# Both triangular solves of the chunked delta rule in rooms of their own, block and bias-row loads on GpSimd, modulation pieces in pairs

## The chip, the cores and the metric

One core of a Trainium2 chip runs the whole program: TensorE (PE) multiplies, VectorE (DVE) and ScalarE (ACT) work on elements, GpSimd (POOL) sets memory and copies, SyncE (SP) issues most of the loads and stores. The metric is the device time of one execution in microseconds (us); the median of several is compared.

## The reference, cut to what matters

The model is a backbone of two layers over 256 latent tokens and 256 context tokens, 2048 wide. Every layer has a mixer and a gated feed-forward block (FFN), each with a shift, a scale and a gate that come from the conditioning vector c. The part of the first layer's mixer that the change touches is a delta rule that runs over chunks of 64 tokens in both directions, first over the context ("ctx", without an output), then from its final states over the latent tokens ("own" below):

```python
sh1, sc1, g1, sh2, sc2, g2 = jnp.split(silu(c) @ ada_w[l] + ada_b[l], 6, axis=-1)
m = jnp.where(i[:, None] > i[None, :], jnp.einsum('bhnid,bhnjd->bhnij', kb, k) * decay, 0.0)
t_inv = lax.linalg.triangular_solve(eye + m, eye, left_side=True, lower=True, unit_diagonal=True)
...
def step(s, xc):
    v_new = u_c - w_c @ s
    s_next = s * jnp.exp(gl_c) + kd_c.T @ v_new
    return s_next, (None if q is None else qd_c @ s + a_c @ v_new)
...
o_c, s_ctx_fin = gdn_bidirectional(None, k_c, v_c, g_c, beta_c, (zeros, zeros))
o_l, _ = gdn_bidirectional(q_l, k_l, v_l, g_l, beta_l, s_ctx_fin)
y_na = neighbourhood_attention(qb, kb, vb, k_ctx_na, v_ctx_na, rpb)     # scores + rows of rpb
y = jnp.concatenate([norm(o_l) * silu(za), y_na], axis=-1) @ w_out
```

All of it is in float32. A product with a weight is made of three matmuls on halves of the operands: high times high, low times high, high times low.

## The kernel before, in words

**The weight stream.** Weights are loaded by SyncE in pieces of 128x1024 (`raw`), split by ACT (`whi`, line 176) and by the DVE (`wlo`, line 250), and used by matmuls at lines 303, 304, 308, 320 and 348. The first layer's stream runs through the segments KA, QA, VA (keys, queries, values of the delta rule), KB0, VB0, KB1, VB1 (keys and values of the attention heads, in halves), QB0, QB1 (their queries), ZA (gate of the delta rule) and WO (output projection); then comes the FFN. One `wlo` serves 24 weight matmuls of the stream up to ZA. "Weight matmul n" or "split n" below counts from the start of this stream.

**The other work** stands in a plan and is fed between the weight matmuls at a pace for each segment: `R_KB` for KB and VB, `R_QB`, `R_ZA`, `R_WO`. `P_CH` and `P_INV` say at which place of the plan the steps of the delta rule begin. The numbers set the program order of each engine, and every engine works through its own order without overtaking.

**The delta rule** goes like this, for ctx and then for own:

- `chunk_matrices` computes the 16 triangular matrices (lines 984 to 1009), cuts out the 32x32 diagonal blocks (`dgs`), the neighbours of size 32 (`n32`, copied by GpSimd at line 1006) and of size 64 (`n64`, by ACT), sends them through DRAM (`nd64`, `nd32`, `dl`), and solves all diagonal blocks at once on the DVE in 31 dependent steps (lines 1030 to 1034, on `lsol` and `zsol`). The solution and its transpose go to DRAM (`dz`).
- `load_diag` sets two tiles to zero on GpSimd (`xd`, `xdT`; lines 1053, 1054) and loads four 32x32 blocks of 16 matrices into each (line 1059, by SyncE): 64 KB a load, in pieces of 32 floats.
- `inverses` builds the inverse of the 128x128 matrices out of the blocks, with small matmuls (lines 1085, 1092, 1098; tiles `gd`).
- `scan` runs the recurrence (lines 1123 to 1167) on `state`.

Tiles with the same tag share room, and the later one waits until the earlier one is no longer read. `nt` (a chunk's matrix) and `lsol` share one room between ctx and own, as do `dgs`, `zsol` and `xd` under the tag "diag".

**Beside it.** `ada_mixer` computes 12 rows of 512 modulation values, each as a sum over 16 pieces: SyncE loads a piece (`araw`, 256 KB, line 433) up to six ahead, the DVE adds it to `acc` (line 438), whose first row was loaded with the bias. A matmul with ones closes a row (line 445). The attention heads need rows of `rpb` as bias: `bq`, loaded by SyncE in two halves for a head (line 1307). GpSimd loads `hC`, a part of the modulated input, in seven loads (line 1276) in the stream's half VB1.

Of the kernel before, what the change touches and what calls it, by code (L numbers as in the profile page):

```python
# [29 lines left out]
D = 2048  # L30
# [12 lines left out]
KH = 2  # L43
P_CH = 2
P_INV = (16, 22, 50, 56)
AB = 6
AHEAD = 6
LAG = 3
LATER = 2
R_QB = 0.6  # L50
R_KB = 1.6
R_ZA = 2.0
R_WO = 2.0
NST = 3
# [58 lines left out]
def body(tc, x, c, ctx, c_ctx, ada_w, ada_b, norm_mix, norm_ffn, ffn_w_gate, ffn_w_up, ffn_w_down,  # L113
# [240 lines left out]

    def ada_done(l, seg, kind, gamma, fs_, p):

        if kind == "sc":
            DVE.scalar_tensor_tensor(scc[l, seg - 1][:, fs_], p, 1.0, gamma[:, fs_], op0=OP.add, op1=OP.mult)
        else:
            DVE.tensor_copy((shc if kind == "sh" else gcol)[l, seg][:, fs_], p)  # L360
# [54 lines left out]
    def ada_mixer(pool_, parts):  # L415


        wr = ada_w[0].rearrange("(k p) n -> p k n", p=128)
        blocks = [(seg, kind, gamma, b) for seg, kind, gamma in parts for b in range(4)]
        accs, raws = {}, {}  # L420

        def load(i):
            n, k = divmod(i, KT)
            if n >= len(blocks):
                return
            seg, b = blocks[n][0], blocks[n][3]
            c0 = seg * D + b * 512
            if not k:
                acc = accs[n] = pool_.tile([128, 512], F32, name="acc", tag="acc", bufs=2)
                DVE.memset(acc, 0.0)  # L430
                SP.dma_start(acc[0:1, :], ada_b[0:1, c0:c0 + 512])
            raws[i] = pool_.tile([128, 512], F32, name="araw", tag="araw", bufs=AB)
            SP.dma_start(raws[i], wr[:, k, c0:c0 + 512])

        def total(i):
            n, k = divmod(i, KT)
            with tc.issue_after(last_lo[0]):
                DVE.scalar_tensor_tensor(accs[n], raws.pop(i), cT[:, k:k + 1], accs[n], op0=OP.mult, op1=OP.add)  # L438

        def close(n):  # L440
            seg, kind, gamma, b = blocks[n]
            acc = accs.pop(n)
            p = smt()
            for f in range(4):
                PE.matmul(p[:, f:f + 1], acc[:, f * 128:(f + 1) * 128], ones[:, 0:1], start=True, stop=True)
            ada_done(0, seg, kind, gamma, slice(b * 4, b * 4 + 4), p[:, 0:4])
            if kind == "row" and b == 3:
                p = smt()
                transpose(p[0:16, 0:128], gcol[0, seg])
                g = pool_.tile([16, 128], F32, name="grow", tag="araw", bufs=AB)  # L450
                DVE.tensor_copy(g, p[0:16, 0:128])
                SP.dma_start(row_d[0, seg], g)

        for i in range(AHEAD):
            load(i)
        N = len(blocks) * KT
        for i in range(N + LAG):
# [109 lines left out]
    ACT.dma_start(vrow[64:112, :], od_conv.rearrange("o t (k p) -> (o t k) p", p=128))  # L567
    brow = sp.tile([32, 128], F32, name="brow")
    bT = sp.tile([128, 32], F32, name="bT")
    ACT.dma_start(brow, ada_b[0:1, 0:4096].rearrange("o (r p) -> (o r) p", p=128))  # L570
    ACT.dma_start(erow, ev_conv.rearrange("o t (k p) -> (o t k) p", p=128))
# [79 lines left out]
    def columns():  # L651
# [7 lines left out]
        p = smt()  # L659
        transpose(p[:, 0:32], brow)  # L660
        DVE.tensor_copy(bT, p[:, 0:32])

    acopy(pick, C("pick"))
    alog = epool.tile([128, 16], F32, name="alog")
    dtb = epool.tile([128, 16], F32, name="dtb")
    gnb = epool.tile([128, 128], F32, name="gnb")


# [204 lines left out]
    brest = epool.tile(gsh, F32, name="brest")  # L873
    epool.tile([128, 48], F32, name="pad_e")

# [50 lines left out]
    flush()  # L926
    state = gw.tile([128, 2, 8, 128], F32, name="state")

# [23 lines left out]
    def load_feat(tag, src, pool_=None, bufs=1):  # L952
        t = (pool_ or gw).tile([128, 1024], F32, name=tag, tag=tag, bufs=bufs).rearrange("p (h t) -> p h t", h=4)
        SP.dma_start(t, src)
        return t

    def chunk_matrices(seq):

# [6 lines left out]
        else:  # L965
            n64 = lgo.tile([128, 1024], F32, name="n64", tag="o_t", bufs=2).rearrange("p (n c) -> p n c", n=16)
            n32 = g4("n32", "vtok")[:, 0:512].rearrange("p (n c) -> p n c", n=16)
            dgs = lgo.tile([128, 1024], F32, name="dgs", tag="o_t", bufs=2)
        dgs = dgs.rearrange("p (n c) -> p n c", n=32)
        for q in range(2):  # L970
# [64 lines left out]
        for d in range(2):  # L1035
            for v in range(2):
                src = (zsol, lsol)[d ^ v][d * 64:(d + 1) * 64].rearrange("p r c -> p (r c)")
                SP.dma_start(dz[v, :, :, d].rearrange("b q t e -> (b q) t e"), src)
        return nd64, nd32, dz

    def load_offdiag(parts):

        n64 = gw.tile([128, 16, 64], F32, name="n64", tag="n64", bufs=1)
        n32 = gw.tile([128, 16, 32], F32, name="n32", tag="n32", bufs=1)
        SP.dma_start(n64, parts[0])
        SP.dma_start(n32, parts[1])
        return n64, n32

    def load_diag(dz, q, tag="diag"):
# [5 lines left out]
        for b in range(4):  # L1055
            s_ = slice(b * 32, b * 32 + 32)
            c_ = slice((b % 2) * 32, (b % 2) * 32 + 32)
            for v, m_ in ((0, xd[s_, :, c_]), (1, xdT[s_, :, s_])):
                SP.dma_start(m_, dz[v, b, q].rearrange("d t (r c) -> r (d t) c", r=32))
        return xd, xdT  # L1060
# [152 lines left out]
    def own_chunks():  # L1213
        nonlocal off, diag, own
        own = chunk_matrices(0)
        off = load_offdiag(parts)
        diag = load_diag(parts[2], 0)

    def first_inverse():
        nonlocal diag  # L1220
        xdTs.append(inverses(off, diag, 0))
        diag = load_diag(parts[2], 1)

    def second_inverse():
        nonlocal off, diag
# [74 lines left out]
    def na_scores(h):  # L1300
# [401 lines left out]
```

## Time and profile before

| | |
|---|---|
| median of 3 executions | 2722.46 us (2722.18 to 2723.68) |
| the profiled execution | 2726.88 us |
| its span on the chip | 2725.1 us |
| granted TensorE clock, mean | 0.992 |
| TensorE busy | 2655.1 us |
| VectorE busy | 1923.7 us |
| data moved | 682.71 MB, mean 251 GB/s |

The profile is of one execution. Its page gives the busy time of each engine, the chain of work that ended last, and the costliest groups of instructions; the trace behind it gives each instruction, what it waited for, and windows of time. In a group's row stand the line of the kernel, the engine, the operation, and output and inputs by their names. "<-" in a wait names what ended it. The granted clock is TensorE's clock as the throttle let it run, 1.00 at full speed.

### The profile page before, as it was taken

The numbers are of one execution on the slowest core, as the hardware profiler recorded it, in microseconds if no ns is written. First come the engines' busy times: TensorE is split into PE (matmuls) and PEld (weight loads), VectorE is DVE, ScalarE is ACT, GpSimd is POOL, SyncE is SP. The second block draws the span as 40 slices with busy tenths as digits, with TensorE's granted clock in tenths as the row PEclk, the third lists the DMA queues.
The fourth block names the chain that finished last, engine by engine and source line by source line (L and its number), as shares of the span: only waits on it lengthen the run. The fifth ranks groups of instructions, "written<-read, shape, count | busy, mean of one in ns | idle before, by whom it ended". The sixth has DMA issues, their size and how long they took to land.

```text
span 2725.1 us, 37531 instructions
## 1 busy us (share of the span) xinstructions
PE 2655.1 (97%) x13775; PEld 2188.7 (80%) x13775; DVE 1923.7 (71%) x2652; ACT 1279.2 (47%) x1851; POOL 47.1 (2%) x73
## 2 busy tenths in 40 slices
PE   6999999999989999999999999999999999999998
PEld 4688888787877888888888878888878888888886
DVE  3378798856678877776788878888575555545675
ACT  3257633244454544444455554444464444445554
POOL 0000101100000000000000000000000000000000
PEclk9999999999999999999999999999999999999999
DMA  9945587986657878888888859997577777666653
GB/s 368 349 156 178 177 278 241 319 266 178 224 220 255 320 274 296 293 300 271 299 282 284 295 161 344 317 337 273 178 234 237 225 239 225 216 195 218 195 193 110
DMA packets 285124, 682.71 MB, mean 251 GB/s; under 512 B 56969, under 2 KB 98545, under 8 KB 283531
## 3 DMA queue, kind: packets, MB, share of 16 engines
q1 hardware_dynamic: 278660, 667.16, 73.1%
q10 hardware_dynamic: 4375, 9.48, 1.0%
q0 software_dynamic: 1904, 3.67, 0.4%
q8 instruction: 108, 1.77, 0.3%
q14 instruction: 77, 0.63, 0.1%
HBM read 658.16 MB, written 22.05 MB: 250 GB/s over the span
## 4 chain that ended last, share of the span: by engine, by line
PE 91%; DMA 3%; DVE 2%; ACT 2%; issue 1%; SPq 1%; DVEq 0%; ACTq 0%
PE mm L303 22%; PE mm L308 21%; PE mm L304 21%; PE mm L348 10%; PE mm L320 8%; PE sm L195 2%; PE sm L599 1%; PE gd L348 1%; DMA bq<-in_ev_rpb_dram 1%; DMA araw<-in_ada_w_dram 1%; PE sm L1337 1%; PE gd L1143 0%; PE gd L942 0%; DMA xn<-in_ctx_dram 0%; DVE wlo L250 0%
## 5 line engine op out<-in xcount | busy, mean ns | idle before, releaser
L250 DVE TENSOR_TENSOR wlo<-raw,whi 128x1024 fp32r<-128x1024 f32 x800 | 971.3, 1221 | 447.9 <-ACT whi L176 437.6
L176 ACT ACTIVATE whi<-raw 128x1024 fp32r<-128x1024 f32 x800 | 843.5, 1062 | 864.2 <-PE mm L308 636.2
L303 PE MATMUL mm<-whi,fhi 128*128 128x512 f32 x1232 | 482.3, 393 | 2.6 <-DVE fhi L1459 2.6
L304 PE MATMUL mm<-wlo,fhi 128*128 128x512 f32 x1232 | 479.8, 390 | 0.5 <-DVE wlo L250 0.5
L308 PE MATMUL mm<-whi,flo 128*128 128x512 f32 x1232 | 389.9, 390 | 0.0
L403 DVE SCALAR_TENSOR_TENSOR acc<-araw,cT,acc 128x1024 f32<-128x1024 f32 x224 | 286.5, 1279 | 37.6 <-DMA araw<-in_ada_w_dram 34.5
L303 PEld LDWEIGHTS mm<-whi,fhi 128*128 128x128 f32 x1232 | 231.6, 188 | 51.2 <-DVE fhi L1459 4.2
L308 PEld LDWEIGHTS mm<-whi,flo 128*128 128x128 f32 x1232 | 231.1, 188 | 48.4
L304 PEld LDWEIGHTS mm<-wlo,fhi 128*128 128x128 f32 x1232 | 231.5, 188 | 47.4 <-DVE wlo L250 0.9
L303 PE MATMUL mm<-whi,ahi 128*128 128x512 f32 x664 | 259.1, 390 | 0.0
L304 PE MATMUL mm<-wlo,ahi 128*128 128x512 f32 x664 | 258.3, 389 | 0.0
L348 PE MATMUL mm<-hB,whi 128*128 128x512 f32 (+1 forms) x840 | 235.3, 366 | 1.0 <-DVE hB L623 1.0
L308 PE MATMUL mm<-whi,alo 128*128 128x512 f32 x664 | 206.6, 389 | 0.0
L348 PEld LDWEIGHTS mm<-hB,whi 128*128 128x128 f32 x840 | 147.7, 189 | 24.3 <-DVE hB L623 2.2
L179 ACT ACTIVATE ahi<-prodT 128x256 fp32r<-128x256 f32 x176 | 73.1, 418 | 182.9 <-PE mm L304 178.1
L438 DVE SCALAR_TENSOR_TENSOR acc<-araw,cT,acc 128x512 f32<-128x512 f32 x192 | 142.4, 745 | 12.2 <-DMA araw<-in_ada_w_dram 10.9
L348 PE MATMUL mm<-hB,wlo 128*128 128x512 f32 (+1 forms) x420 | 149.5, 364 | 0.0
L308 PEld LDWEIGHTS mm<-whi,alo 128*128 128x128 f32 x664 | 124.6, 188 | 26.0
L303 PEld LDWEIGHTS mm<-whi,ahi 128*128 128x128 f32 x664 | 124.7, 188 | 25.7
L304 PEld LDWEIGHTS mm<-wlo,ahi 128*128 128x128 f32 x664 | 124.7, 188 | 25.5
L303 PE MATMUL mm<-whi,dhi 128*128 128x512 f32 x336 | 131.2, 393 | 1.2 <-DVE dhi L1459 1.2
L304 PE MATMUL mm<-wlo,dhi 128*128 128x512 f32 x336 | 130.8, 390 | 0.0
(422 smaller groups left out, 3530.3 us busy)
## 6 DMA issues: line engine op xcount, KB each, us to landing
araw<-in_ada_w_dram SPq DMA_DIRECT2D x288, 512.0 KB
raw<-in_ffn_w_down_dram SPq DMA_DIRECT2D x176, 512.0 KB
raw<-in_ffn_w_gate_dram SPq DMA_DIRECT2D x160, 512.0 KB
raw<-in_ffn_w_up_dram SPq DMA_DIRECT2D x160, 512.0 KB
raw<-in_ev_w_in_dram SPq DMA_DIRECT2D x112, 512.0 KB
araw<-in_ada_w_dram SPq DMA_DIRECT2D x192, 256.0 KB
raw<-in_od_w_in_dram SPq DMA_DIRECT2D x96, 512.0 KB
raw<-in_ev_w_out_dram SPq DMA_DIRECT2D x32, 512.0 KB
```

The lines of the kernel that those rows point to most:

```text
L176: ACT.activation(dst, src, AF.Copy)
L179: ACT.activation(hi, src, AF.Copy)
L195: return PE.transpose(dst, src, ident[:n, :n])
L250: last_lo[0] = DVE.tensor_tensor(lo, raw, hi, op=OP.subtract).ins
L303: PE.matmul(ps[ti][n], a, hi[:, n * 512:(n + 1) * 512], start=first, stop=False)
L304: ins = PE.matmul(ps[ti][n], a, lo[:, n * 512:(n + 1) * 512], start=False, stop=False).ins
L308: last_mm[0] = PE.matmul(ps[ti][n], b, hi[:, n * 512:(n + 1) * 512], start=False, stop=False).ins
L320: ins = PE.matmul(ps[ti][n], a(t), w[:, c_], start=False, stop=a is ll and hi is group[-1][0]).ins
L348: last_mm[0] = PE.matmul(o, wt, h_(slice(0, len(ws)), mv, k), start=i == 0 and g == 0 and j == 0, stop=i == len(ks) - 1 and g == len(group ...
L403: DVE.scalar_tensor_tensor(acc, raw, cT[:, k:k + 1], acc, op0=OP.mult, op1=OP.add)
L438: DVE.scalar_tensor_tensor(accs[n], raws.pop(i), cT[:, k:k + 1], accs[n], op0=OP.mult, op1=OP.add)
L599: ins = PE.matmul(pr[32 * j:32 * j + 32, :], cT2[:, g + j, :], raw[:, j].rearrange("p s n -> p (s n)"), start=g == 0, stop=g == KT - 4).ins
```

## The change

- **Rooms.** `nt` and `lsol` of the own chunks move to a tile `room` in the place that `state` takes later, and the solve's scratch to a tile `half`; `state` is allocated after the second ctx inverse. So the own solve doesn't wait for the room of the ctx solve. `n64` and `n32` of ctx stay on the chip and no longer go through DRAM, nor does `n64` of own; `n32` of own still does.
- **Blocks.** Both halves (q = 0, 1) of the ctx blocks are loaded at once. The loads of `load_diag` (32) and of `bq` (16) are issued by GpSimd in place of SyncE.
- **Modulation.** Two pieces come in one load of 512 KB. The first piece of a row is a product without a sum, so no clearing of `acc` and no bias load; the bias is added when the row closes, from `bM`, which a larger `brow` and one more copy provide at the start.
- **Paces.** `P_CH`, `P_INV`, `R_QB`, `R_KB`, `R_ZA`, `R_WO`.

The diff, without lines that only pass a name on:

```diff
-P_CH = 2
-P_INV = (16, 22, 50, 56)
+P_CH = 1
+P_INV = (20, 26, 44, 50)
-R_QB = 0.6
-R_KB = 1.6
-R_ZA = 2.0
-R_WO = 2.0
+R_QB = 1.5
+R_KB = 1.0
+R_ZA = 3.0
+R_WO = 1.6
...
-    def ada_done(l, seg, kind, gamma, fs_, p):
+    def ada_done(l, seg, kind, gamma, fs_, p, bias=None):
-        if kind == "sc":
+        if bias is not None:
+            dst = scc[l, seg - 1] if kind == "sc" else (shc if kind == "sh" else gcol)[l, seg]
+            DVE.tensor_tensor(dst[:, fs_], p, bias, op=OP.add)
+            if kind == "sc":
+                DVE.scalar_tensor_tensor(dst[:, fs_], dst[:, fs_], 1.0, gamma[:, fs_], op0=OP.add, op1=OP.mult)
+        elif kind == "sc":
...
-                acc = accs[n] = pool_.tile([128, 512], F32, name="acc", tag="acc", bufs=2)
-                DVE.memset(acc, 0.0)
-                SP.dma_start(acc[0:1, :], ada_b[0:1, c0:c0 + 512])
-            raws[i] = pool_.tile([128, 512], F32, name="araw", tag="araw", bufs=AB)
-            SP.dma_start(raws[i], wr[:, k, c0:c0 + 512])
+                accs[n] = pool_.tile([128, 512], F32, name="acc", tag="acc", bufs=2)
+            if k % 2:
+                return
+            raw = pool_.tile([128, 2, 512], F32, name="araw", tag="araw", bufs=AB // 2)
+            SP.dma_start(raw, wr[:, k:k + 2, c0:c0 + 512])
+            for j in range(2):
+                raws[i + j] = raw[:, j, :]
...
-                DVE.scalar_tensor_tensor(accs[n], raws.pop(i), cT[:, k:k + 1], accs[n], op0=OP.mult, op1=OP.add)
+                if k:
+                    DVE.scalar_tensor_tensor(accs[n], raws.pop(i), cT[:, k:k + 1], accs[n], op0=OP.mult, op1=OP.add)
+                else:
+                    DVE.tensor_scalar(accs[n], raws.pop(i), cT[:, 0:1], None, op0=OP.mult)
...
-    state = gw.tile([128, 2, 8, 128], F32, name="state")
+    room = gw.tile([128, 2, 1024], F32, name="ntl", tag="state", bufs=1)
+    state = None
...
-                nt = gw.tile([128, 2, 4, 128], F32, name="nt", tag="lsol", bufs=1)
+                nt = (gw.tile([128, 2, 4, 128], F32, name="nt", tag="lsol", bufs=1) if seq else
+                      room[:, 0, :].rearrange("p (d i e) -> p d i e", d=2, i=4))
...
-        lsol = g4("lsol", "lsol").rearrange("p (r c) -> p r c", r=32)
-        nd64 = dram.tile([128, 16, 64], F32, name="nd64", tag="nd64", bufs=2)
-        nd32 = dram.tile([128, 16, 32], F32, name="nd32", tag="nd32", bufs=2)
-        SP.dma_start(nd64, n64)
-        SP.dma_start(nd32, n32)
+        lsol = (g4("lsol", "lsol") if seq else room[:, 1, :]).rearrange("p (r c) -> p r c", r=32)
+        if seq:
+            half.append(g4("half", "vtok"))
+        else:
+            SP.dma_start(nd32, n32)
+            n32 = None
...
-        sub_tmp = g2("sub_tmp").rearrange("p i e -> p (i e)")
+        sub_tmp = half[0][:, 512 + seq * 256:768 + seq * 256]
...
             for v, m_ in ((0, xd[s_, :, c_]), (1, xdT[s_, :, s_])):
-                SP.dma_start(m_, dz[v, b, q].rearrange("d t (r c) -> r (d t) c", r=32))
+                POOL.dma_start(m_, dz[v, b, q].rearrange("d t (r c) -> r (d t) c", r=32))
...
         own = chunk_matrices(0)
-        off = load_offdiag(parts)
-        diag = load_diag(parts[2], 0)
+        off = parts[:2]
+        diag = [load_diag(parts[2], q, ("diag", "kT")[q]) for q in range(2)]
...
-        xdTs.append(inverses(off, diag, 0))
-        diag = load_diag(parts[2], 1)
+        xdTs.append(inverses(off, diag[0], 0))
...
-        xdTs.append(inverses(off, diag, 1))
+        xdTs.append(inverses(off, diag[1], 1))
+        state = gw.tile([128, 2, 8, 128], F32, name="state", tag="state", bufs=1)
...
-        off = load_offdiag(own)
-        diag = [load_diag(own[2], q, ("diag", "kT")[q]) for q in range(2)]
+        off = own_offdiag(own[0])
+        diag = [load_diag(own[2], q, ("diag", "n64")[q]) for q in range(2)]
...
-            SP.dma_start(bq[half * 64:half * 64 + 64], src)
+            POOL.dma_start(bq[half * 64:half * 64 + 64], src)
```

The lines of the changed kernel are up to 16 higher: the blocks are loaded at line 1075 (before 1059), `hC` at 1291 (1276), the first product of `inverses` is line 1101 (1085), a modulation piece line 446 (438). What each engine has to do, in its order, with the semaphores that a row waits for (DMAHW for loads by SyncE or ACT, DMASW for loads by GpSimd, with the number of the semaphore):

On GpSimd before, from the end of the own chunk's copies to `hC`; the blocks are not in its order.

```order
L1006 COPY n_3273<-nt 32x128 [waits DVE_49]
L1006 COPY n_3273<-nt 32x128
L1023 MEMSET dgs 128x1024 [waits DVE_49,PE_49,DMAHW6_49,Activation_49,Pool_49]
L1024 MEMSET dgs 128x32 [waits Pool_49]
L1053 MEMSET xd 128x1024 [waits DMAHW3_49,DMAHW2_49,DMAHW4_49,DVE_49,PE_49]
L1276 DMA hC<-h_d 128x2x512 [waits PE_49]
L1276 DMA hC<-h_d 128x2x512 x6
```

On GpSimd now, from the last memset ahead of the ctx blocks to the memsets (lines 1041 and 1042) for the own solve's `zsol`, which lies in the room named dgs:

```order
L1069 MEMSET xd 128x1024 [waits DMAHW2_49,DMAHW3_49,DVE_49,Pool_49]
L1075 DMA xdT<-dz 32x16x32 [waits DMAHW4_49]
L1075 DMA xdT<-dz 32x16x32 x7
L1075 DMA xd<-dz 32x16x32 [waits DMAHW5_49,DMASW0_49,Pool_49]
L1075 DMA xd<-dz 32x16x32 [waits DMASW1_49]
L1075 DMA xd<-dz 32x16x32 [waits DMASW2_49]
L1075 DMA xd<-dz 32x16x32 [waits DMASW3_49]
L1023 COPY half<-ntl 32x128 [waits DVE_49]
L1023 COPY half<-ntl 32x128
```

The 16 ctx blocks come as twelve ahead of the last quarter of the copies of the own chunk's `n32` (here `half`), and four more behind them; the four loads of `xd`, which the first inverse reads, are the ninth to the twelfth.

On TensorE before, the first product of the first ctx inverse, in KB1 ahead of weight matmul 1668:

```order
L348 MATMUL mm<-hB_105,wlo 128x512
L1085 MATMUL gd<-xd,n_3620 32x32 [waits DMAHW2_49,DMAHW3_49,DVE_49,Pool_49]
L1085 MATMUL gd<-xd,n_3620 32x32 [waits DMAHW4_49]
L1085 MATMUL gd<-xd,n_3620 32x32 [waits DMAHW3_49]
L1085 MATMUL gd<-xd,n_3620 32x32 x29
```

And now the end of the same product, in VB0, between weight matmuls 1487 and 1493:

```order
L1101 MATMUL gd<-xd,n_1581 32x32 [waits DMASW2_49]
L1101 MATMUL gd<-xd,n_1581 32x32 [waits DMASW1_49]
L308 MATMUL mm<-whi,hB_105 128x512
L303 MATMUL mm<-whi,hB_105 128x512 [waits Activation_49]
L304 MATMUL mm<-wlo,hB_105 128x512 [waits DVE_49]
L1101 MATMUL gd<-xd,n_1581 32x32 [waits DMASW3_49]
L1101 MATMUL gd<-xd,n_1581 32x32 x28
```

The product has moved ahead by some 175 weight matmuls and waits for loads by GpSimd; each row of it stands ahead of weight matmuls that are ready.

On the DVE before, behind the last sum of modulation pieces but one, while WO ends and the norm of the FFN's input is formed (`nx0`, `nx1`: its factors for the two halves of the tokens; `xs` the stream's sum, `rtmp` and `xc` the scaled rows, `fhi` and `flo` the halves of the FFN's input):

```order
L1402 TENSOR_REDUCE ss_7657<-ssx 128x1
L219 TENSOR_SCALAR nx1v<-ss_7657 128x1
L221 RECIPROCAL nx1r<-nx1s 128x1
L222 TENSOR_TENSOR nx1s<-nx1r 128x1
L223 SCALAR_TENSOR_TENSOR nx1s<-nx1s,nx1v 128x1
L224 SCALAR_TENSOR_TENSOR nx1r<-nx1s,nx1r 128x1
L1447 TENSOR_SCALAR xc<-xs,nx1r 128x512
```

And now at the same place:

```order
L1408 TENSOR_TENSOR xs<-rtmp,xs 128x512
L446 SCALAR_TENSOR_TENSOR acc<-araw,cT,acc 128x512 x2
L1417 TENSOR_REDUCE ss_7477<-ssx 128x1
L446 SCALAR_TENSOR_TENSOR acc<-araw,cT,acc 128x512
L219 TENSOR_SCALAR nx1v<-ss_7477 128x1
L446 SCALAR_TENSOR_TENSOR acc<-araw,cT,acc 128x512
L221 RECIPROCAL nx1r<-nx1s 128x1
L446 SCALAR_TENSOR_TENSOR acc<-araw,cT,acc 128x512
L222 TENSOR_TENSOR nx1s<-nx1r 128x1
L446 SCALAR_TENSOR_TENSOR acc<-araw,cT,acc 128x512
L223 SCALAR_TENSOR_TENSOR nx1s<-nx1s,nx1v 128x1
```

Of the 192 pieces, 18 now stand behind the split numbered 146, where two stood.

More of the change, by code (lines that the diff above doesn't have):

```diff
@@ L445, in close @@
                 PE.matmul(p[:, f:f + 1], acc[:, f * 128:(f + 1) * 128], ones[:, 0:1], start=True, stop=True)
-            ada_done(0, seg, kind, gamma, slice(b * 4, b * 4 + 4), p[:, 0:4])
+            m0 = (seg - 2) * 16 + b * 4
+            ada_done(0, seg, kind, gamma, slice(b * 4, b * 4 + 4), p[:, 0:4], bM[:, m0:m0 + 4])
             if kind == "row" and b == 3:
@@ L449, in close @@
                 transpose(p[0:16, 0:128], gcol[0, seg])
-                g = pool_.tile([16, 128], F32, name="grow", tag="araw", bufs=AB)
+                g = pool_.tile([16, 128], F32, name="grow", tag="araw", bufs=AB // 2)
                 DVE.tensor_copy(g, p[0:16, 0:128])
@@ L567, in body @@
     ACT.dma_start(vrow[64:112, :], od_conv.rearrange("o t (k p) -> (o t k) p", p=128))
-    brow = sp.tile([32, 128], F32, name="brow")
+    brow = sp.tile([80, 128], F32, name="brow")
     bT = sp.tile([128, 32], F32, name="bT")
-    ACT.dma_start(brow, ada_b[0:1, 0:4096].rearrange("o (r p) -> (o r) p", p=128))
+    ACT.dma_start(brow, ada_b[0:1, 0:5 * D].rearrange("o (r p) -> (o r) p", p=128))
     ACT.dma_start(erow, ev_conv.rearrange("o t (k p) -> (o t k) p", p=128))
@@ L659, in columns @@
         p = smt()
-        transpose(p[:, 0:32], brow)
+        transpose(p[:, 0:80], brow)
         DVE.tensor_copy(bT, p[:, 0:32])
+        DVE.tensor_copy(bM, p[:, 32:80])
     acopy(pick, C("pick"))
@@ L666, in body @@
     gnb = epool.tile([128, 128], F32, name="gnb")
+    bM = epool.tile([128, 48], F32, name="bM")
     scale = HD ** -0.5
@@ L873, in body @@
     brest = epool.tile(gsh, F32, name="brest")
-    epool.tile([128, 48], F32, name="pad_e")
     def gates():
@@ L955, in load_feat @@
         return t
+    half = []
+    nd32 = dram.tile([128, 16, 32], F32, name="nd32")
     def chunk_matrices(seq):
@@ L966, in chunk_matrices @@
             n64 = lgo.tile([128, 1024], F32, name="n64", tag="o_t", bufs=2).rearrange("p (n c) -> p n c", n=16)
-            n32 = g4("n32", "vtok")[:, 0:512].rearrange("p (n c) -> p n c", n=16)
+            n32 = half[0][:, 0:512].rearrange("p (n c) -> p n c", n=16)
             dgs = lgo.tile([128, 1024], F32, name="dgs", tag="o_t", bufs=2)
@@ L1038, in chunk_matrices, with own_offdiag @@
                 SP.dma_start(dz[v, :, :, d].rearrange("b q t e -> (b q) t e"), src)
-        return nd64, nd32, dz
-    def load_offdiag(parts):
-        n64 = gw.tile([128, 16, 64], F32, name="n64", tag="n64", bufs=1)
+        return n64, n32, dz
+    def own_offdiag(n64):
         n32 = gw.tile([128, 16, 32], F32, name="n32", tag="n32", bufs=1)
-        SP.dma_start(n64, parts[0])
-        SP.dma_start(n32, parts[1])
+        SP.dma_start(n32, nd32)
         return n64, n32
@@ L1215, in own_chunks @@
         own = chunk_matrices(0)
-        off = load_offdiag(parts)
-        diag = load_diag(parts[2], 0)
+        off = parts[:2]
+        diag = [load_diag(parts[2], q, ("diag", "kT")[q]) for q in range(2)]
     def first_inverse():
-        nonlocal diag
-        xdTs.append(inverses(off, diag, 0))
-        diag = load_diag(parts[2], 1)
+        xdTs.append(inverses(off, diag[0], 0))
     def second_inverse():
-        nonlocal off, diag
-        xdTs.append(inverses(off, diag, 1))
+        nonlocal off, diag, state
+        xdTs.append(inverses(off, diag[1], 1))
+        state = gw.tile([128, 2, 8, 128], F32, name="state", tag="state", bufs=1)
         for q in range(2):
```

## The prediction

> **What bounds the kernel now.** I read the page first: busy shares (part 1), then the chain that ended last (part 4).
>
> ```profile
> span 2725.1 us, 37531 instructions
> PE 2655.1 (97%) x13775; PEld 2188.7 (80%) x13775; DVE 1923.7 (71%) x2652; ACT 1279.2 (47%) x1851; POOL 47.1 (2%) x73
> PE 91%; DMA 3%; DVE 2%; ACT 2%; issue 1%; SPq 1%; DVEq 0%; ACTq 0%
> ```
>
> TensorE is busy for 97% of the span and carries 91% of the chain. The change takes no matmul of the weight stream away, so all that it can win is TensorE's idle time, and all that it can lose is new idle time. What it rewrites runs from about 400 to 885 us, so the windows of that stretch and TensorE's waits in it come next. Columns of the windows: length; busy us of PE, PEld, DVE, ACT, POOL; then the granted TensorE clock, the DMA share and GB/s.
>
> ```profile
> 400.00:480.00 80.00, 78.91 (x466) 66.65 (x465) 69.52 (x135) 25.79 (x45) 7.87 (x17) 0.98 0.77 247
> 560.00:640.00 80.00, 69.72 (x784) 64.73 (x783) 46.81 (x89) 32.32 (x64) 4.58 (x3) 0.96 0.80 230
> 720.00:800.00 80.00, 71.15 (x391) 60.12 (x390) 49.64 (x110) 45.65 (x110) 0.00 (x0) 0.96 0.48 167
> 800.00:880.00 80.00, 76.38 (x337) 62.92 (x336) 72.62 (x109) 31.42 (x46) 0.00 (x0) 0.96 0.81 292
> ...
> 560.00:580.00 20.00, 15.50 (x117) 15.10 (x115) 8.51 (x17) 5.38 (x8) 1.81 (x1) 0.91 0.73 199
> 620.00:640.00 20.00, 15.96 (x380) 14.35 (x367) 10.10 (x22) 8.76 (x16) 0.00 (x0) 1.00 0.69 192
> 760.00:780.00 20.00, 13.09 (x67) 9.75 (x67) 12.35 (x41) 15.20 (x53) 0.00 (x0) 0.92 0.13 48
> 860.00:880.00 20.00, 16.38 (x65) 13.05 (x64) 15.29 (x37) 6.69 (x16) 0.00 (x0) 0.83 0.38 127
> ```
>
> ```profile
> PE sm L1337 <- DVE PT L173: 4.4, 2, 3.7
> PE mm L348 <- DVE wlo L250: 4.4, 1, 4.4
> PE sm L445 <- DVE acc L438: 3.2, 1, 3.2
> PE gd L1143 <- DMA vtok<-vd__151: 1.9, 1, 1.9
> ...
>   DMA bq<-in_ev_rpb_dram: 32.5, 8
> ```
>
> From 400 to 480 TensorE is nearly full (78.9 of 80). The idle time lies behind: 10.3 us in 560–640, 8.9 in 720–800, 3.6 in 800–880. After a gap the granted clock drops too: 0.91, 0.92 and 0.83 over 20 us are 1.8, 1.6 and 3.4 us more. The gaps on wlo and on PT (4.4 each) stand behind the last row, the DVE's idle time at the bias rows bq: 32.5 us in 8 waits. The DVE works in order, so the weight split wlo and the products PT behind such a wait come late. The idle time of 720–800 is the end of the last recurrence scans, where no weight matmuls are left to fill in.
>
> **Part 1, what can be won.** (a) The 16 loads of bq leave SyncE's queue, where each stood among modulation and weight loads, for GpSimd's, where those of the first three heads stand together and the later ones wait only for a free buffer. Of the PT gap I count all (4.4; the clock of 620–640 stays at 1.00), of the wlo gap at the first head a third with its clock, 2. (b) The own scan ends while ZA's matmuls run, so the bare stretch goes: 8.9 idle and 1.6 of clock, of which I count 9, since 16 transposes of o_t still stand together after it. (c) The vtok wait (1.9) with some of the 0.91 clock: 2.5. Sum **−18**. Bounds: 0, if each gap is replaced by a wait of the same kind, and −23, if all of the two windows and their clock go (10.3 + 8.9 + 1.8 + 1.6).
>
> **Part 2, what is new on the path.** GpSimd now issues the 16 context blocks xd and xdT, and TensorE's first inverse, L1101, stands among the weight matmuls 1465 to 1493 of the stream, where before L1085 came at 1668, in a later stage. These rows show both issuers (start, us, line, tile, count; in brackets the idle time before).
>
> ```profile
> 410.06 1.23 SPq L1038 DMA_DIRECT2D dz<-lsol  x2
> 416.06 0.87 SPq L1059 DMA_DIRECT2D xdT<-dz  x2
> 420.30 2.61 SPq L1059 DMA_DIRECT2D xdT<-dz  x5
> ...
> 412.42 0.96 POOL L1053 MEMSET xd<- 128x1024 f32 x1 [38.53 <-DMA dz<-zsol]
> 527.70 2.25 POOL L1276 DMA_DIRECT2D hC<-h_d  x3 [21.08 <-PE mm L308]
> 534.03 0.72 POOL L1276 DMA_DIRECT2D hC<-h_d  x1 [4.07 <-issue]
> 535.28 0.71 POOL L1276 DMA_DIRECT2D hC<-h_d  x1 [0.54 <-issue]
> 536.52 0.71 POOL L1276 DMA_DIRECT2D hC<-h_d  x1 [0.52 <-issue]
> 542.32 0.71 POOL L1276 DMA_DIRECT2D hC<-h_d  x1 [5.09 <-issue]
> ...
> q0 software_dynamic: 1904, 3.67, 0.4%
> ...
> xd<-dz SPq DMA_DIRECT2D x16, 64.0 KB
> ```
>
> GpSimd's queue holds little. Of seven hC loads three are issued at once; the fourth comes 6.33 us after the first (534.03 − 527.70), the seventh 8.29 us after the fourth, each with idle time that no semaphore ends ("issue"). The queue's 1904 packets are 272 for each load, 17 on each of 16 DMA engines: three loads (51) fit, four (68) don't. A block of 64 KB moves in pieces of 32 × 4 = 128 bytes, 512 of them, 32 on each engine and presumably one more that signals, as hC has 17 for 16. Two blocks make 66, so unless the limit is exactly 66 or 67 the blocks go **one at a time**: a block has to land before the next is issued.
>
> The time T of one block. Three hC loads at 1.25 us apiece (the spacing of 534.03, 535.28, 536.52) explain 3.75 of the 6.33 us until the first room; the other 2.6 is a load's fixed part, the low end. The high end is that 6.33 itself. Between: SyncE issued five blocks in 2.61 us, 0.52 each, so 3.1 without other traffic; the DMA engines are busy to 0.77 here with loads of far larger packets, and between the last hC issues, in a busier stretch (the fourth load took 2 us longer than the first), more was added. I take **T = 4**, nearer the low end.
>
> When they start. Before, zsol's stores gave way to the memset of xd at 412.42 and to the first block at 416.06. The context solve stands one or two weight splits earlier on the DVE now, but the DVE carries more there: 69.5 of 80 us before, and 14 more modulation pieces up to the 60th split. I take 410 for the first issue (bounds 405 and 416). The inverse needs the 9th block at its first matmul and the 12th at weight matmul 1493. That one runs at 425 before; by the order 52 matmuls of own chunk matrices have been moved ahead of it, at about 1.1 us for eight 7 us:
>
> ```profile
> 424.79 0.39 PE L304 MATMUL mm<-wlo,hB 128*128 128x512 f32 x1
> 427.83 1.13 PE L942 MATMUL gd<-cs,gm 128*128 128x128 f32 x8
> 428.80 1.06 PE L984 MATMUL gd<-kT 128*128 128x128 f32 x8
> ```
>
> So TensorE arrives at 432 and the 12th block lands at 410 + 12 × 4 = 458: **+26**, plus 2 of lowered clock after such a gap, as after those above. Bounds: T = 2.6 gives 441, +9; T = 6.3 gives 486, +54. The weight matmuls behind the waiting inverse are ready but can't pass it. Before, the same blocks had some 55 us (423 to the 1668th matmul) to land, which is the cover that is gone.
>
> Also behind those 12 issues on GpSimd: the copies into half, hence the store of n32 on SyncE, and behind it three of the own lsol loads and the next weight loads. SyncE stalls until about 457, but splits up to the 67th are loaded by then and TensorE is at the 63rd, 4 splits of some 6 us away; I price it at 0, up to +8 at T = 6.3. The memset that the own solve needs stands behind 16 blocks, 410 + 64 = 474; the solve stands at split 65, which TensorE wants at 432 + 28 + 15 = 475. No further loss at T = 4, 5 to 10 at T = 6. The own blocks, hC and bq follow in the same queue, with the own scans later by the same 28 us as everything on TensorE.
>
> By the Trainium skill, "DMA: Bandwidth & Descriptors", section "Anatomy of one DMA — SWDGE (gpsimd) path", a GpSimd load takes about 2.0 us and its bytes at 436 GB/s; an estimate from it for 64 KB is 2.15 us, hence a stall of 4 in place of 26 if the blocks went one by one. The same page, section "SWDGE vs HWDGE vs iDMA", says that each engine takes turns between this path and SyncE's. The row of 8.29 us for three loads agrees with the second and not with an unloaded figure.
>
> **Part 3, modulation pieces.** The column sum of a piece (L438) costs 745 ns on the DVE:
>
> ```profile
> L438 DVE SCALAR_TENSOR_TENSOR acc<-araw,cT,acc 128x512 f32<-128x512 f32 x192 | 142.4, 745 | 12.2 <-DMA araw<-in_ada_w_dram 10.9
> ```
>
> There are 192 before and after. The 12 memsets and 12 bias loads that go were on queues with room, as are the bias additions that come: 0. Loads of 512 KB in pairs bring the same bytes: 0, ±2. But 18 pieces stand after the 146th split, where there were 2: 16 × 0.745 = 12 us more DVE work among the last residual sums, the norm and its casts, in a window where the DVE had 7.4 us to spare (72.62 of 80) and TensorE already waits 3.2 for the last sum at a clock of 0.83. I take **+4**; bounds −3 (that wait goes) and +12 (all of it shows). The stores and loads of n64 that fall away (four transfers) were off the path: 0.
>
> **Sum.** −18 + 26 + 2 + 4 = +14 on the profiled execution's 2726.9 (span 2725.1 and 1.8 around it), so 2741; that execution is 4.4 above the median of 2722.5, so **2736**.
>
> **Rivals.** *No stall, and faster.* Two blocks fit in the queue, or hand-over overlaps: 6 pairs in some 4 us each land at 434, and the stall is 2 or less. Then −18 + 4 = −14 on the median, 2708. For it: the count 66 is close to what is known to fit, 51 to 67, and SyncE's own rate, 0.52 a block. Against it: the idle time between hC loads. *The page's price or the low end.* One at a time in 2.6 us: −18 + 9 + 1 + 4 = −4, 2718, and with T = 3.1 (stall 15) some 2724: no change. *Long blocks.* At T of 5.5 to 6.3 each small packet waits for a large one: stall 44 to 54, and SyncE, the own solve and the first bq come late too: −14 + 49 + 3 + 4 + 6 = +48, but the longer stall lets the DVE get ahead, −10: 2760. It decides from T = 5. *The change does not do what it says*: the own solve could still wait for the context's end. In the order it runs between splits 65 and 70, five after the context's; only the memset of part 2 ties them, so this is in the bounds.
>
> **How the numbers follow.** Forecast (T of 3.3 to 5, one at a time) 0.43, own range 2727 to 2752; long blocks 0.13; cancelling 0.18; no stall 0.26. What a measurement can tell from no change is about 0.2%, 5.4 us. Slower by more: 0.43 + 0.13 = 0.56; within: 0.18; faster: 0.26. The range leaves a tenth out on each side: 2704, a little below the no-stall case, to 2768, above the long one.
>
> **What would show it.** Right: one TensorE gap of 20 to 30 us at L1101, near 430 to 460, released by a load of xd; L1075 issues on GpSimd 3 to 5 us apart with idle time ended by "issue"; fewer bq waits on the DVE; no bare stretch before 800. Wrong: L1075 issues in one burst, or a gap below 10 us; then the stall is gone and the sum falls below the median. If the sum is right but the gaps of 560–800 remain, the gains were mis-sized; if TensorE waits at L455 or at fhi near 880 for more than 8 us, part 3 was.

## The result, and the profile after

The changed kernel takes 2770.0 us (median of 4, 2767.8 to 2774.2), the kernel before 2722.3 in the same runs: a ratio of 1.0177, 95% interval 1.0159 to 1.0194. It is **slower by 48 us**; the forecast was 2736, and its range ended at 2768. The profiled execution has a span of 2768.7 us, 43.6 more than before.

The page of the changed kernel, span and busy time of the engines:

```profile
span 2768.7 us, 37244 instructions
PE 2660.5 (96%) x13775; PEld 2192.4 (79%) x13775; DVE 1917.4 (69%) x2645; ACT 1282.1 (46%) x1852; POOL 80.9 (3%) x121
```

TensorE's busy time grew by 5.4 us (2655.1 before; 13775 matmuls in both, at a mean granted clock of 0.983 in place of 0.992), so 38 of the 43.6 us are idle time. Stages as in the prediction, with the columns explained there; first the two of the kernel before that the prediction doesn't show, then the changed kernel:

```profile
640.00:720.00 80.00, 78.97 (x612) 66.80 (x611) 57.62 (x107) 34.22 (x73) 0.00 (x0) 0.98 0.72 220
880.00:960.00 80.00, 79.19 (x364) 65.59 (x363) 64.38 (x69) 45.01 (x64) 0.96 (x1) 1.00 0.85 304
...
400.00:480.00 80.00, 52.83 (x446) 43.28 (x445) 39.44 (x86) 16.90 (x30) 17.32 (x29) 0.81 0.54 154
560.00:640.00 80.00, 65.45 (x864) 58.95 (x864) 41.89 (x70) 23.46 (x41) 14.69 (x20) 0.91 0.88 255
640.00:720.00 80.00, 74.01 (x531) 67.97 (x526) 62.81 (x129) 35.70 (x90) 5.33 (x8) 0.96 0.82 236
720.00:800.00 80.00, 79.11 (x411) 65.07 (x410) 53.28 (x112) 42.11 (x100) 1.32 (x2) 1.00 0.47 132
880.00:960.00 80.00, 69.80 (x299) 56.84 (x298) 67.10 (x106) 35.11 (x63) 0.96 (x1) 0.87 0.72 259
```

TensorE's idle time is 27.2 us in 400–480 (before 1.1), 14.6 in 560–640 (10.3), 6.0 in 640–720 (1.0), 0.9 in 720–800 (8.9) and 10.2 in 880–960 (0.8). The bare stretch of the scans is gone, as forecast; far more has come in the other four. What TensorE waited for from 380 to 960, and the DVE's longest waits (from 400):

```profile
PE gd L1101 <- DVE xd L1116: 19.6, 2, 11.2
PE gd L1101 <- DMA xd<-dz: 18.8, 1, 18.8
PE sm L455 <- DVE acc L446: 7.9, 2, 5.4
...
DVE wlo L250 <- ACT whi L176: 76.9, 33, 24.4
DVE bq L1324 <- DMA bq<-in_ev_rpb_dram: 34.5, 7, 11.0
DVE half L1047 <- POOL dgs L1042: 11.8, 1, 11.8
```

The timeline of GpSimd (start, us, line, operation; idle time before and what ended it):

```profile
412.39 0.78 POOL L1075 DMA_DIRECT2D xdT<-dz  x1 [1.80 <-DMA dz<-lsol]
417.80 0.66 POOL L1075 DMA_DIRECT2D xdT<-dz  x1 [4.63 <-issue]
...
436.45 0.65 POOL L1075 DMA_DIRECT2D xdT<-dz  x1 [1.91 <-issue]
439.04 0.66 POOL L1075 DMA_DIRECT2D xdT<-dz  x1 [1.94 <-issue]
...
449.34 0.66 POOL L1075 DMA_DIRECT2D xd<-dz  x1 [1.93 <-issue]
450.04 1.27 POOL L1023 COPY half<-ntl 32x128 f32<-32x128 f32 x4
...
466.37 0.17 POOL L1042 MEMSET dgs<- 128x32 f32 x1
```

Twelve blocks go out one by one between 412.4 and 449.3, 3.36 us apart on average, with idle time that no semaphore ends. TensorE came to the first inverse at 425.1 and stood until 444.0, when the ninth block had landed: 18.8 us. What GpSimd has to do behind the blocks came late with them, as the DVE's and SyncE's timelines show:

```profile
427.23 1.53 DVE L446 SCALAR_TENSOR_TENSOR acc<-araw,cT,acc 128x512 f32<-128x512 f32 x2
453.13 1.23 DVE L250 TENSOR_TENSOR wlo<-raw,whi 128x1024 fp32r<-128x1024 f32 x1 [24.37 <-ACT whi L176]
454.27 0.48 DVE L448 TENSOR_SCALAR acc<-araw,cT 128x512 f32<-128x512 f32 x1
466.58 0.20 DVE L1047 TENSOR_TENSOR half<-ntl,dgs 128x31 f32<-128x31 f32 x1 [11.82 <-POOL dgs L1042]
...
423.70 5.09 SPq L1038 DMA_DIRECT2D ntl<-dl  x6
451.34 0.34 SPq L1031 DMA_DIRECT2D nd<-half  x1
```

SyncE issues nothing from 429 to 451, since the store of `half` waits for the copies at 450.0. The own solve (L1047) starts at 466.6, when the memset of L1042, which stands behind all 16 blocks, is done. Line L1116, which writes the result of the first inverse's 32x32 products into `xd`, stands behind the first steps of that solve in the DVE's order, and TensorE waits for it before the 64x64 products of the same inverse, 8.4 us from 465.3:

```profile
473.66 0.44 PE L1101 MATMUL gd<-xd,n 64*64 64x64 f32 x2 [8.36 <-DVE xd L1116]
```

(The texts on record ahead of the runs call this the wait at the second context inverse; that one starts at 484.5 and doesn't wait.) The other 11.2 us of the row of L1116, from 620.5, are the same place in the second own inverse, and there it is the bias rows: they come behind the own blocks and `hC` in GpSimd's order, the first goes out at 610.1, and the DVE, which has L1116 behind them, waits for them until 616.8, again until 621.4 and until 628.7.

### The profile page after: what moved, and what is told of

Read it like the earlier page. It is cut to its first block, busy times and chain, and to the rows that moved or that the text cites. A ratio compares the mean times of both kernels' runs of the same rounds, so it can differ in the third digit from the quotient of the medians.

```text
span 2768.7 us, 37244 instructions
## 1 busy us (share of the span) xinstructions
PE 2660.5 (96%) x13775; PEld 2192.4 (79%) x13775; DVE 1917.4 (69%) x2645; ACT 1282.1 (46%) x1852; POOL 80.9 (3%) x121
## 4 chain that ended last, share of the span: by engine, by line
PE 74%; DMA 3%; DVE 3%; issue 1%; POOL 0%; ACT 0%; SPq 0%; DVEq 0%; POOLq 0%; ACTq 0%
PE mm L303 21%; PE mm L304 20%; PE mm L308 20%; PE mm L320 7%; PE sm L195 2%; PE mm L348 1%; DMA araw<-in_ada_w_dram 1%; DMA bq<-in_ev_rpb_dram 1%; DVE acc L446 1%; DMA raw<-in_ev_w_out_dram 1%; DVE wlo L250 0%; PE gd L1159 0%; PE sm L1352 0%; DMA qT<-qTd 0%; PE gd L1167 0%
## 5 line engine op out<-in xcount | busy, mean ns | idle before, releaser
L446 DVE SCALAR_TENSOR_TENSOR acc<-araw,cT,acc 128x512 f32<-128x512 f32 x180 | 134.6, 748 | 4.5 <-DMA araw<-in_ada_w_dram 3.0
```

## The experiments

Each ratio is to the kernel before on the same chip.

### Memory of GpSimd's queue, and who issues

```diff
-    nc = _bacc.Bacc("TRN2", target_bir_lowering=False, num_devices=1, dynamic_dma_scratch_size=1024)
+    nc = _bacc.Bacc("TRN2", target_bir_lowering=False, num_devices=1, dynamic_dma_scratch_size=1536)
```

> The changed kernel with 1536 bytes of descriptor memory for GpSimd's queue in place of 1024, every engine's order the same. Theory Q (the queue holds one block of 33 packets for each DMA engine, so a block has to land before the next is issued, 3.4 us each, and three waits of TensorE follow from it: 18.8 us at the first context inverse, 8.4 at the second behind the own solve's memset, 11.2 at the second own inverse behind late bias rows): two blocks fit, they go out in pairs, the 12th is issued near 432 in place of 449, the first wait falls from 18.8 to 2 to 8 us, the other two to under 5 each, and the time to 2735 to 2750. Rival B (the DMA engines shared with SyncE's loads set the 3.4 us): two at once take twice as long each, the waits stay, and the time stays above 2762.

2742.1 us, ratio 1.0077 (1.0062 to 1.0092), 28 under the changed kernel with every instruction in the same place. GpSimd's timeline of this run:

```profile
413.38 1.43 POOL L1075 DMA_DIRECT2D xdT<-dz  x2 [1.77 <-DMA dz<-lsol]
419.61 1.30 POOL L1075 DMA_DIRECT2D xdT<-dz  x2 [4.80 <-issue]
423.09 1.30 POOL L1075 DMA_DIRECT2D xdT<-dz  x2 [2.17 <-issue]
...
447.67 0.17 POOL L1042 MEMSET dgs<- 128x32 f32 x1
```

The blocks now go mostly in pairs, and the memset comes at 447.7 in place of 466.4. What TensorE still waits for at L1101:

```profile
PE gd L1101 <- DMA xd<-dz: 9.0, 1, 9.0
PE gd L1101 <- DVE xd L1116: 3.4, 1, 3.4
```

The wait at the first inverse is 9.0 us (18.8), the one before its 64x64 products is gone, the one in the second own inverse is 3.4 (11.2). So the room of the queue sets the pace: theory Q. The first wait was a little over what was expected, since two of the pairs still took 6.2 and 5.5 us.

The next three move issues back to SyncE, the blocks (`e1_blocks_sp`), the bias rows (`e2_bq_sp`), both (`e3_both_sp`):

```diff
-                POOL.dma_start(m_, dz[v, b, q].rearrange("d t (r c) -> r (d t) c", r=32))
+                SP.dma_start(m_, dz[v, b, q].rearrange("d t (r c) -> r (d t) c", r=32))
...
-            POOL.dma_start(bq[half * 64:half * 64 + 64], src)
+            SP.dma_start(bq[half * 64:half * 64 + 64], src)
```

> The changed kernel with the 32 block loads issued by SyncE again; the bias rows bq and hC stay with GpSimd. The first context inverse moves a little ahead, to weight matmul 1455. Theory Q: with GpSimd's queue free of blocks all three waits go (18.8, 8.4, 11.2) and about 5 us of lowered clock, while blocks in SyncE's queue cost up to 8 at the first inverse: 2725 to 2740. Rival S (the early place of the inverse and of the own solve is what costs, whoever issues): a wait of over 15 us stays at the first inverse, and the time stays above 2750.

> The changed kernel with the 16 bias-row loads issued by SyncE again, the blocks still by GpSimd; TensorE's order is the same. Theory Q: the wait at the second own inverse (11.2 us, behind DVE waits for bq of 11.0, 2.3 and 5.3) shrinks to what the bias rows cost before the change, about 4 to 5; the waits at the two context inverses stay at 18.8 and 8.4: 2760 to 2766. Rival S: the third wait stays as it is, since the last blocks xdT come just as late, and the time with it: 2768 to 2772.

> The changed kernel with blocks and bias rows both issued by SyncE again; what is left of the change is the rooms, the pairs of pieces and the paces. Theory Q: about as with the blocks alone on SyncE, plus the old waits at the bias rows, some 4 to 8 us more than that run: 2730 to 2745. Against the kernel before (2722) the rest then says what the earlier own solve, the paces and the modulation pieces cost or bring without GpSimd's queue; by the prediction's terms -9 (bare stretch), -2.5 and +4, so 2715, by the trace of the changed kernel (6 to 8 us of new waits for the last modulation sums, 2.7 for qT) rather 2725.

Blocks on SyncE: 2737.9, ratio 1.0057 (1.0042 to 1.0072). Bias rows on SyncE: 2755.9, ratio 1.0123 (1.0108 to 1.0138); the two waits of the first inverse stay (19.1 and 8.0 us), the 11.2 are gone, and more came back than expected, as the DVE's waits for bias rows fell to 19.8 us. Both: 2737.2, ratio 1.0053 (1.0036 to 1.0070). With the blocks on SyncE there is no wait at the first inverse in either run, though it stands ten weight matmuls earlier. And with the blocks out of the way it makes no difference to the time who issues the bias rows. The DVE's waits for them don't get shorter, though: 32.8 us with GpSimd as their issuer and no block in its queue, 30.1 with SyncE; only the longest single wait does (7.6 and 5.5 us, 11.0 in the changed kernel). So the blocks explain the late first rows, and not the sum of these waits. Taken out of the changed kernel, GpSimd's queue is worth 33 of the 48 us.

### One part alone, and the place of the inverse

The kernel before with the blocks issued by GpSimd, and nothing else (`e7_before_pool`); and the changed kernel with later places alone (`e15_after_later`):

```diff
-P_INV = (20, 26, 44, 50)
+P_INV = (40, 46, 58, 64)
```

> The kernel before with one part of the change alone: the 32 block loads issued by GpSimd, everything else as it was (bias rows on SyncE, old paces and rooms, first inverse at weight matmul 1668). Theory Q: 8 blocks at 3.4 us each from 412 are there by 440, TensorE needs them near 480, so the first inverse doesn't wait; the second block pair (8 more, after the first inverse) and hC behind them may wait up to 10 us at the second inverse or at hC: 2720 to 2735. Rival S: GpSimd's loads cost as in the changed kernel, over 2745.

> The changed kernel (blocks and bias rows by GpSimd) with later places alone, P_INV (40, 46, 58, 64): the first context inverse at weight matmul 1632 in place of 1465, some 45 us later. Theory R (TensorE's wait for the blocks was only the first in line; GpSimd, in order and stuck at 16 issues until 466, also holds the copies into half and the memset of the own solve, and with them the DVE and SyncE): the wait of 18.8 at the inverse goes, but a wait of 10 to 25 us for a weight split or the own solve takes its place near 435 to 470, the bias rows come late as before, and the time is 2750 to 2766. Rival E (the early place of the inverse was the fault): no wait over 6 us between 420 and 500, 2735 to 2748.

`e7_before_pool`: 2756.2, ratio 1.0131 (1.0116 to 1.0146), outside what theory Q was thought to allow and in the range of rival S (over 2745). `e15_after_later`: 2773.5, ratio 1.0191 (1.0175 to 1.0206), no better than the changed kernel, and above both theories' ranges. The waits of TensorE and of the DVE, first in the one and then in the other:

```profile
PE gd L195 <- DVE nt L987: 22.3, 1, 22.3
DVE nt L987 <- POOL n L1006: 21.5, 1, 21.5
...
PE mm L348 <- DVE wlo L250: 30.9, 2, 25.4
DVE half L1047 <- POOL dgs L1042: 31.3, 1, 31.3
```

In neither does TensorE wait for a block at its first ctx inverse (in the first it does at later ones, 4.3 us in all near 545 and 8.3 near 675). In the first the DVE can't write the next own matrix, since GpSimd's copy of the last one (L1006) stands behind twelve blocks; in the second the DVE stands 31.3 us before the own solve, whose memset is behind sixteen, and the weight splits with it. So theory Q had the cause and was priced too narrowly: **what costs is that GpSimd, in order, stands still at the issues**, with other engines' work behind it as well as the blocks themselves. The wait at the inverse was only the first in line, and moving it away puts the next in its place.

### Paces and modulation pieces

`e6_kb` is `e3_both_sp` with one number, `e8_pool_kb` the changed kernel with the same:

```diff
-R_KB = 1.0
+R_KB = 1.6
```

> Blocks and bias rows issued by SyncE, as in e3_both_sp, and R_KB back at 1.6. By the order all 192 modulation pieces are done at split 132 (e3_both_sp: 148 of 192, with 28 behind split 146), and the first context inverse stands at weight matmul 1540 in place of 1455. Theory P (the slower pace over KB and VB pushed the pieces into the end of WO, where e3_both_sp waits 9.6 + 2.9 + 2.1 + 1.0 us at a clock of 0.88 to 0.94): those waits fall below 3 us together, and the time from 2737 to 2718 to 2726. Rival D (the pieces only move the DVE's overload from the end of WO to KB, VB and QB): new waits of over 8 us between 400 and 700 us, and the time stays above 2731.

> The changed kernel (blocks and bias rows issued by GpSimd, 1024 bytes of descriptor memory) with R_KB back at 1.6 alone. The first context inverse moves from weight matmul 1465 to 1607, some 40 us later, and no piece is left at the end of WO. Theory Q and P together: the 12th block has landed at about 452 and TensorE comes near 465, so no wait at the first inverse (18.8 before), less than 3 at the second, bias rows still late behind the own blocks and hC (5 to 11 us), no waits at the end of WO (10.2 before): 2725 to 2740. Rival S (GpSimd's loads cost wherever they stand): 2750 or more.

`e6_kb`: 2729.8, ratio 1.0032 (1.0021 to 1.0044), 7 under `e3_both_sp`, which waited in the end of WO like this:

```profile
PE sm L455 <- DVE acc L446: 11.6, 2, 9.6
PE mm L303 <- DVE fhi L1474: 4.0, 2, 2.9
```

Of those 15.6 us 1.2 in two waits are left in `e6_kb`, as in the kernel before, so theory P holds for the place. But 6.3 us come back where the own scans end; first `e3_both_sp`, then `e6_kb`:

```profile
720.00:800.00 80.00, 79.43 (x387) 65.45 (x386) 58.01 (x104) 47.08 (x94) 0.00 (x0) 0.98 0.58 212
720.00:800.00 80.00, 73.10 (x372) 60.14 (x371) 58.57 (x117) 47.24 (x97) 0.00 (x0) 0.94 0.61 209
```

TensorE's idle time there is 6.9 us in place of 0.6, while from 400 to 720 it hardly changes (19.1 and 20.2). So the slow pace that rid the end of the scans of its bare stretch is the one that filled the end of WO, and the time missed its range. `e8_pool_kb`: 2749.2, ratio 1.0106 (1.0089 to 1.0123), missed too, just under the 2750 of rival S. The earlier pieces push the ctx solve back on the DVE, the first block goes out at 441 and not at 412, and TensorE waits 14.2 us at the later inverse and 15.9 behind the bias rows.

`e9_pairs` is the kernel before with the modulation part of the diff alone, `e11_bias` the same with the pieces still loaded one by one (no clearing, bias at the close):

> The kernel before with the modulation part of the change alone: pieces in pairs of 512 KB, no clearing of acc, bias added at the close; old paces, rooms and issuers. By the prediction this part by itself is worth 0, +-2: 2719 to 2725. Rival: a pair that lands as one load comes later than its first piece did and the DVE waits for it (the DVE's waits for araw were 8.7 us before), 2728 or more.

> The kernel before with the bias part of the modulation edit alone: no clearing of acc, bias added at the close from the chip, pieces still loaded one by one. Theory L (the pairs cost): 2717 to 2723, as the kernel before. Rival O: 2726 to 2732, as e9_pairs.

`e9_pairs`: 2730.1, ratio 1.0033 (1.0021 to 1.0045). `e11_bias`: 2724.2, ratio 1.0008 (0.9999 to 1.0018). So the bias part is free within what these runs can tell, and the pairs cost some 6 to 7 us in this program. Why isn't settled, as the trace is of the fastest of the six executions (2726.0): the DVE's waits for pieces are no longer (10.3 us against 10.9), the waits that are new are short ones for a block, a staging tile and two scan products, and the pairs also change the order in which work is set. Between `e6_kb` and `e10_single` (below) they cost nothing.

### What is left without GpSimd's queue

`e10_single` is `e6_kb` with the pieces one by one; `e12_bq_act` has the bias rows issued by ACT besides; `e14_later` adds P_INV (40, 46, 58, 64); `e13_before_bq_act` is the kernel before with the bias rows issued by ACT.

```diff
-            SP.dma_start(bq[half * 64:half * 64 + 64], src)
+            ACT.dma_start(bq[half * 64:half * 64 + 64], src)
```

> Blocks and bias rows issued by SyncE, R_KB 1.6, as in e6_kb (2729.8), and the modulation pieces loaded one by one (256 KB, six ahead) as before the change; the bias still comes at the close. What is left of the change is the rooms with the earlier own solve, the bias from the chip, the places P_INV and the other paces. Theory L (the pair loads cost the 9 us of e9_pairs and the same here, since a load of 512 KB holds small urgent loads back in SyncE's queue and a pair's room comes free only when both pieces are used): 2717 to 2724. Rival O (e9_pairs lost its 9 us by the other parts of the modulation edit, or by the new order of the program): 2727 to 2732 as e6_kb.

> As e10_single, with the bias rows issued by ACT in place of SyncE: a queue that holds neither GpSimd's small ring nor SyncE's weight loads. If the DVE's waits for bias rows (23.7 us in e6_kb) are the time that a load stands behind others in SyncE's issue order, they fall below 10 us and the time is 3 to 8 us under that of e10_single. If they are the time of the transfer itself (7 us for each load, whoever issues), or ACT, which works in order, gets stuck at an issue, no gain: within 3 us of e10_single, or above it.

> As e12_bq_act (blocks by SyncE, bias rows by ACT, single pieces, R_KB 1.6; 2730.5), with P_INV (40, 46, 58, 64): the first context inverse at weight matmul 1632 in place of 1536. If the 8 us by which e10_single and e12_bq_act stay above the kernel before are the waits at the early inverse (5.5 us for a block, 3.5 for a staging tile behind it, a clock of 0.89 in 400 to 480), they go: 2717 to 2723. If they come from elsewhere in the earlier own solve and scans: 2726 to 2732, with the waits moved.

> The kernel before with one edit alone: bias rows issued by ACT in place of SyncE. The DVE waited 32.5 us for them, and TensorE 8 to 9 us behind it. If issue order was the cause: DVE waits for bq below 12 us, 2712 to 2718. If the transfer itself is: 2719 to 2726.

`e10_single`: 2730.8, ratio 1.0041 (1.0029 to 1.0054): theory L falls here. `e12_bq_act`: 2730.5, ratio 1.0035 (1.0022 to 1.0047): the DVE's waits for bias rows are 16.7 us, little under the 18.7 of `e10_single`, and no time is won. Both wait at the first inverse, 5.3 and 5.5 us, and for a staging tile behind it. `e14_later`: **2722.1, ratio 0.9998 (0.9989 to 1.0007)**; the inverse 96 weight matmuls later, and the 8 us are gone. It is the best form of the change found, and it stands where the kernel before stands.

`e13_before_bq_act`: 2719.2, ratio 0.9996 (0.9987 to 1.0005). The DVE's waits for bias rows fell from 32.5 to 15.4 us, so about half of them was the place in SyncE's queue:

```profile
DVE bq L1309 <- DMA bq<-in_ev_rpb_dram: 15.4, 6, 4.1
```

In its profile TensorE's idle time from 300 to 960 is 23.5 us against 27.0, but the interval includes no gain. No run here is faster than the kernel before beyond its interval.

## Why the prediction was wrong, point by point

- **One block at a time: right, on an untested assumption.** The 17 of a `hC` load are packets as the profile counts them, the 33 of a block are pieces of 128 bytes and one more. In GpSimd's queue the profile counts 2 packets for a block on each DMA engine, not 33 (last section), and by packets many blocks would have fitted. That the room goes by pieces was taken for granted; the single blocks here and the pairs of `e4_ring1536` bear it out.
- **T = 4, from 410: near.** It was 3.36 us from 412.4. The bounds of 2.6 and 6.3 come out as two regimes: 2.5 to 2.6 us while SyncE stood still, 3.4 to 5.4 while its loads ran. The stall was 18.8 us where +26 stood in the sum: TensorE came at 425, and the ninth block, not the twelfth, ended it.
- **"No further loss at T = 4": the step that failed.** The prediction named the copies, the store, the memset and the bias rows behind the blocks and priced them at 0, because TensorE was to be late by as much. They cost 8.4 us at the own solve and 11.2 at the bias rows, and lowered clock on top (0.66 in 620–640). The memset came at 466, even earlier than the 474 of the prediction; but the solve behind it was priced by the weight split that TensorE wants at 475, and L1116, which stands behind the solve too, was wanted at 465. What matters is that GpSimd is held for 54 us (412 to 466) and again from 516 to 622, and everything in its order with it. T lay inside the 3.3 to 5 of the forecast, and the time outside its own range of 2727 to 2752: with 19.6 of the 34 us between forecast and result, this term is the largest part of the miss.
- **Gains of 18: half failed.** The bare stretch of 720–800 went from 8.9 us idle to 0.9, near the 9 counted. The bias rows brought nothing: 34.5 us of DVE waits in place of 32.5, and still 32.8 in `e1_blocks_sp` without a block ahead of them. The waits of 640–720 are new (6.0 us against 1.0). And the gain of the bare stretch isn't apart from the loss of the next point, as the sum took it: with R_KB back at 1.6 and SyncE issuing the blocks (`e6_kb`, `e10_single`, `e12_bq_act`, `e14_later`) 720–800 has 5.6 to 6.9 us of idle time again. From 300 to 960 TensorE is idle for 28.4 us in `e14_later`, 27.0 before: even without the queue the earlier solve wins nothing.
- **Modulation pieces, +4 with a bound of +12: mis-sized.** 880–960 lost 10.2 us in place of 0.8 (with 3.0 in the stretch ahead of it, 3.6 before), at a clock of 0.87: some 9 us of idle time. `e6_kb` confirms cause and place. The text was also wrong in one remark: up to the 60th split the changed program has 13 pieces fewer, not 14 more; just that delay fills the end of WO.
- **The long-blocks rival (2760) came nearest**, but in part by luck: its condition, T of 5.5 to 6.3, didn't hold; that the own solve and the first bias rows come late did, already at 3.36.

The sum by runs: blocks and bias rows back to SyncE −33 (2770.0 to 2737.2), R_KB −7 (2729.8), pairs ±1 (2730.8), bias rows to ACT 0 (2730.5), a later inverse −8 (2722.1). That is the 48 us, from runs on several chips, on which the kernel before read 2720.6 to 2722.7. The shares hold for this order alone: on the changed kernel itself R_KB is worth 21 us (`e8_pool_kb`), and the later inverse nothing (`e15_after_later`).

## What to carry to other kernels

Before loads are moved to another engine's queue, count how many pieces of a load that queue holds and what else stands in that engine's order: an issue that has to wait for room holds every copy and memset behind it, and through them engines that need none of the loads. Moving the one consumer that shows the wait doesn't help, as `e15_after_later` shows; more room helped (28 us), and an engine that does little but issue, as SyncE here, helped more (33). And when pieces of side work are paced more slowly, look at where the rest of them ends up: what one number won at the end of the scans it lost at the end of WO.

## What the runs showed of the hardware

A GpSimd load of 64 KB in 512 pieces took 2.6 us from issue to issue even where the DMA engines were all but idle. Two windows of the changed kernel, with blocks going out in both:

```profile
413.00:430.00 17.00, 12.14 (x66) 10.18 (x64) 13.02 (x25) 4.67 (x9) 2.14 (x4) 0.94 0.87 237
430.00:450.00 20.00, 6.04 (x19) 4.85 (x20) 0.00 (x0) 0.00 (x0) 5.23 (x8) 0.54 0.11 25
```

In the second the DMA share is 0.11 and they move 25 GB/s; the blocks come 2.6 us apart. In the first, at 0.87, they come 3.4 to 5.4 us apart. The DVE, too, is busy in the first and idle in the second; two windows of `e15_after_later` tell the two apart:

```profile
452.60:461.00 8.40, 0.00 (x0) 0.00 (x0) 0.00 (x0) 0.00 (x0) 1.33 (x4) 0.50 0.86 278
539.50:542.10 2.60, 2.60 (x20) 2.40 (x19) 2.19 (x3) 0.68 (x2) 0.65 (x1) 1.00 0.10 28
```

With the DVE idle and a DMA share of 0.86 the blocks come 4.4 and 4.0 us apart, with a busy DVE and a share of 0.10 they come 2.6 apart. So in these windows the pace goes with the load on the DMA engines, not with the DVE.

With 1024 bytes of descriptor memory one such block was under way, with 1536 two, and of `hC` three and five loads. The rows of the queues, SyncE's (q1) in the changed kernel and in `e1_blocks_sp`, GpSimd's (q0) in `e7_before_pool`, and `hC` with 1536 bytes:

```profile
q1 hardware_dynamic: 252940, 660.83, 70.9%
q1 hardware_dynamic: 269836, 662.93, 72.4%
q0 software_dynamic: 2928, 5.77, 0.7%
552.14 3.50 POOL L1291 DMA_DIRECT2D hC<-h_d  x5 [9.46 <-PE mm L308]
```

The 32 blocks are 16896 packets by SyncE, 33 for a block on each of 16 engines, and 1024 by GpSimd (2928 less the 1904 of `hC`), 2 for a block on each. The room fits a count in pieces: 51 (three `hC`) go and 66 (two blocks) don't with 1024 bytes, 85 (five `hC`) go and 99 (three blocks) don't with 1536. A count in the packets of q0 doesn't fit, as two blocks would be 4 against the 51 of three `hC`.

By the Trainium skill, "DMA: Bandwidth & Descriptors", section "Anatomy of one DMA — SWDGE (gpsimd) path", 64 KB take 2.15 us by estimate; the quiet regime, 2.6 us from issue to issue, is near that, the one beside SyncE's loads isn't. The same page of the Trainium skill, section "Issuing engines are not separate DMA queues", says that a second issuing engine only saves the time that an issue takes on its sequencer. Here the second engine lost time: `e7_before_pool` moves nothing but the issuer and is 1.3% slower.
